# Weight products of a two-layer diffusion trunk as single matmuls on plain float32 operands, in place of three passes over split operands

## The chip, the core and the metric

The kernel runs on one core of one Trainium2 chip. The metric is the device time of one execution in microseconds (us), the median of several runs. Its engines are TensorE (PE in the profile, its weight loads PEld), VectorE (DVE), ScalarE (ACT), GpSimd (POOL) and SyncE (SP), which issues nearly all DMAs.

## The reference

Two layers are applied to 1152 tokens (128 context tokens and 1024 latent grid tokens, nine tiles of 128) of width 1024. Each layer is:

```
m = silu(c) @ w_ada + b_ada                  -> sh1, sc1, g1, sh2, sc2, g2
z = (x * (1 + sc1) + sh1) @ w_in             (1024 -> 2336: HGRN, MLA and GQA parts)
mixed = [HGRN2 scan | MLA attention | GQA attention]
x = layernorm(ALPHA * x + g1 * (mixed @ w_out))
gate, up = (x * (1 + sc2) + sh2) @ w_ffn_in  (1024 -> 2 x 2816)
x = layernorm(ALPHA * x + g2 * ((silu(gate) * up) @ w_ffn_out))
```

Context tokens attend to themselves alone; latent tokens attend to 128 cached tokens and to all latent tokens. All inputs, outputs and weights are float32.

## The kernel before

A layer goes through four stages, in code `phase_b` to `phase_e`.

- In-projection and HGRN (`phase_b`). Activations lie transposed in `HT`, three tiles of 8 feature blocks x 384 tokens. The part `hq` is made in feature layout: 6 accumulations of 8 products with 384 moving columns. Seven further chunks of 256 columns and one of 288 are made token tile by token tile (`token_chunk`): 9 accumulations of 8 products each. The HGRN scan over nine blocks (`hgrn`) runs among them; each block has eight levels, each of which goes through VectorE, ScalarE, GpSimd, TensorE and VectorE again (lines 628 to 657), and these levels' matmuls (line 652) as well as those of lines 676, 679 and 686 are on plain float32 tiles already.
- Attention (`phase_c`): 24 + 24 groups of two query tiles; scores (line 799), softmax, turned probabilities (line 820), products with the values (line 869). Small weight products of MLA stand among them.
- Output projection (`phase_d`): two halves x nine token tiles x 8 products with 512 moving columns, the first norm, and `make_hT`, which turns and modulates the activations for the next stage.
- Feed-forward (`phase_e`): 22 blocks of 128 hidden features. `inp` makes gate and up: 2 x 3 accumulations of 8 products with 384 moving columns per block. `outp` adds the down projection of a pair of blocks: 18 accumulations with 512 moving columns.

The adaLN products (`ada`, a generator) are called between these pieces with `fill`: the parts 2 to 5 of the first layer in the first `phase_b` (64 products with 512 moving columns), all six of the second layer in the first `phase_e` (96 products). The parts 0 and 1 of the first layer come at the start (`ada0`, 32 products).

Precision is kept by splitting. `wsplit` (line 121) loads a weight tile into one of two `raw` buffers, ScalarE rounds it to float32r (line 103), and VectorE or GpSimd subtracts to get the rest (line 104); activations are split in the same way where they are made. `mm3` (line 106) issues three matmuls for each product:

```
nc.tensor.matmul(out, ah, bh, start=i == 0, stop=False)
nc.tensor.matmul(out, ah, bl, start=False, stop=False)
nc.tensor.matmul(out, al, bh, start=False, stop=i == n - 1)
```

For the adaLN products two matmuls do, since the four stationary columns hold both halves of the two condition vectors (line 184); a small matmul with `fold` adds them up (lines 193 and 201). Line 193 is called for two parts x two halves x two layers, eight times; its operands are plain float32, with 4 partitions, 2 stationary and 512 moving columns.

The order of the instructions on each engine comes from a scheduler that works by a simulated timeline of the program as it stands, so that a change of any instruction can move others. A matmul on PE waits in that order, and what is behind it waits with it.

Of the kernel before, what the change touches and what calls it, by code (L numbers as in the profile page):

```python
# [34 lines left out]
# per phase the eighths of a turned tile (mod 4) whose scaling and rounding VectorE does, and whose rest Pool does  # L35
HT_MODES = {"start": ((1, 3), (1,), (1, 3)), "D": ((1, 3), (1,), (1, 3)), "E": ((1, 3), (1,), (1, 3))}
# [17 lines left out]
class Build:  # L54
# [43 lines left out]
    def split(self, hi, lo, src, eng=None, vec=False):  # L98
        """hi = src rounded to float32r, lo = the exact rest."""
# [30 lines left out]
    def setup(self):  # L130
        nc, A = self.nc, self.A
        self.open("dram", space=DRAM)
        for p in ("const", "raw", "wsp", "M", "tmp", "small"):
            self.open(p)
# [5 lines left out]
        self.fold = self.t(c, [4, 2], tag="fold")  # L140
# [3 lines left out]
        cs = self.t(c, [P, 8, 2], tag="cs")  # L144
        nc.scalar.activation(cs, cT, AF.Silu)
        self.cs = self.t(c, [P, 160], F32R, tag="csr")
        nc.vector.memset(self.cs.bitcast(F32), 0.0)
        v = self.cs[:, :32].rearrange("p (k c) -> p k c", c=4)
        self.split(v[:, :, 0:2], v[:, :, 2:4], cs)
# [3 lines left out]
    def floors(self):  # L153
        """the second layer's lower bounds of the gates, and one minus them."""
# [19 lines left out]
    def ada(self, l, part):  # L174
        """part: 0 sh1, 1 sc1, 2 g1, 3 sh2, 4 sc2, 5 g2. A generator of eight pieces of work."""
        nc, A = self.nc, self.A
        for h in range(2):
            acc = self.ps("D")
            c0 = part * D + h * 512
            for k in range(0, 8, 2):  # L180
                hi, lo = self.wsplit(A["w_ada"][l, k * P:(k + 2) * P, c0:c0 + 512].rearrange("(a p) c -> p a c", p=P), [2, 512])
# [5 lines left out]
            m = self.tmp()  # L187
            nc.vector.tensor_copy(m[0:4, :], acc[0:4, :])
            if part in (2, 5):
                r = self.tmp()  # L190
                nc.sync.dma_start(r[0:2, :], A["b_ada"][l:l + 1, c0:c0 + 512].broadcast_to([2, 512]))
                o = self.ps("D")
                nc.tensor.matmul(o[0:2, :], self.fold, m[0:4, :], start=True, stop=True)
                nc.vector.tensor_tensor(r[0:2, :], r[0:2, :], o[0:2, :], op=ALU.add)
                nc.sync.dma_start(self.gd[l][part // 3][:, h * 512:(h + 1) * 512], r[0:2, :])
                continue
            bias = self.t("small", [P, 4], tag="bada", bufs=2)
            nc.sync.dma_start(bias, A["b_adaT"][l, :, part * 8 + 4 * h:part * 8 + 4 * h + 4])
            o = self.ps("D")
            for j in range(4):  # L200
                nc.tensor.matmul(o[:, 2 * j:2 * j + 2], m[0:4, j * P:(j + 1) * P], self.fold, start=True, stop=True)
# [6 lines left out]
    def ada0(self):  # L208
        """the first layer's sh1 and sc1."""
# [4 lines left out]
        def finish(part, h, m):  # L214
            o = self.ps("D")
            for j in range(4):
                nc.tensor.matmul(o[:, 2 * j:2 * j + 2], m[0:4, j * P:(j + 1) * P], self.fold, start=True, stop=True)
# [6 lines left out]
        for part in range(2):  # L224
            for h in range(2):
                acc = self.ps("D")
                c0 = part * D + h * 512
                for k in range(0, 8, 2):
                    w = self.t("st", [P, 2, 512], tag="w", bufs=16)
                    nc.sync.dma_start(w, A["w_ada"][0, k * P:(k + 2) * P, c0:c0 + 512].rearrange("(a p) c -> p a c", p=P))  # L230
                    hi, lo = (self.t("st", [P, 2, 512], F32R, tag=g, bufs=2) for g in "hl")
                    self.split(hi, lo, w)
                    for a in range(2):
                        for x in (hi, lo):
                            nc.tensor.matmul(acc, self.cs[:, 4 * (k + a):4 * (k + a) + P], x[:, a],
                                             start=k + a == 0 and x is hi, stop=k + a == 7 and x is lo)
                    if k == 0 and todo:
                        finish(*todo)
                if part == 0 and h == 0:
                    nc.sync.dma_start(self.ident, A["ident"])  # L240
                    nc.sync.dma_start(self.still, A["still"])
                    nc.sync.dma_start(self.fold, A["fold"])
                    nc.sync.dma_start(bias, A["b_adaT"][0, :, 0:16])
                m = self.tmp()
                nc.vector.tensor_copy(m[0:4, :], acc[0:4, :])
# [8 lines left out]
    def coefs(self, l, which, ln):  # L254
        """(scale, shift) [P, 8, 2] of the modulation; with ln = (layer, norm) that norm's gain and bias are in them."""
# [12 lines left out]
    def make_hT(self, coefs, ci, xt, dst, phase):  # L268
# [3 lines left out]
        vec, hi, pool = HT_MODES[phase]  # L272
        for k in range(8):
# [3 lines left out]
            tm = self.tmp("tu"[k % 2])  # L277
            segs = [(0, P, 0), (P, 384, 1)] if ci == 0 else [(0, 384, 1)]
            for a, b, v in segs:
                if k % 4 in vec:  # L280
                    nc.vector.tensor_scalar(tm[:, a:b], ps[:, a:b], sc[:, k, v:v + 1], sh[:, k, v:v + 1],
                                            op0=ALU.mult, op1=ALU.add)
                else:
                    nc.scalar.activation(tm[:, a:b], ps[:, a:b], AF.Identity, scale=sc[:, k, v:v + 1], bias=sh[:, k, v:v + 1])
# [3 lines left out]
    def hts(self, t, k, a):  # L288
        return self.HT[t // 3][:, k, a, (t % 3) * P:(t % 3 + 1) * P]

# [1 line left out]
    def stats(self, u):  # L292
        """one over the deviation, and the mean, of the rows."""
# [10 lines left out]
    def norm(self, u):  # L304
        """layer norm without gain and bias, in place."""
# [6 lines left out]
    def ln_rows(self, ln):  # L312
        """gain and bias rows of a norm on all partitions [P, 2, D]."""
# [4 lines left out]
    def gate_rows(self, l, gi, dst):  # L318
        """dst [P, 2, D]: the gate rows of both vectors on all partitions."""
# [1122 lines left out]
```

## Time and profile before

| | |
|---|---|
| median of 3 runs | 4151.19 us (4141.76 to 4161.65) |
| profiled execution, first to last instruction | 4234.5 us |
| PE busy | 3772.9 us (89%) |
| DVE, ACT, POOL busy | 53%, 37%, 31% |
| HBM read and written | 231.05 MB, 38.87 MB (64 GB/s over the span) |

The profiled execution has no other time of its own than its span; it is 83 us over the median of the runs. Of the first layer, the in-projection and HGRN lie at about 60 to 460 us of the span, the attention at 460 to 1170, the output projection at 1170 to 1290, the feed-forward at 1290 to 2180; the second layer follows at about 2180, 2570, 3260 and 3400.

In the profile's rows for PE a matmul's duration is from its start to the modelled end of its pipeline, so that the durations of successive matmuls overlap. How long one holds the engine is the distance between two successive starts. A granted clock (PEclk) of 1.00 is 2.4 GHz and 0.50 is 1.2 GHz; a stretch with a value between has had both.

### The profile page before, as it was taken

The page shows a single profiled execution, that of the slowest core. Times are in us where ns is not written, and L with a number is a line of the kernel's source. Part 1 is how long each engine was busy: PE and PEld are TensorE (multiplying, and loading weights), DVE is VectorE, ACT ScalarE, POOL GpSimd, SP SyncE. Part 2 cuts the span into 40 slices and gives each one's busy share as a digit, 9 for nine tenths or more (in the row PEclk, how much of TensorE's full clock was granted, in tenths as well). Part 3 has the DMA queues.
Part 4 walks back from the last instruction along what each step waited for, and adds up shares of the span by engine and source line. Part 5 has one row for each costly group of instructions (what it writes and reads, how often), then busy time and mean ns, then how long its engine had stood idle before and what let it go on. Part 6 is the DMA issues. An engine that isn't in the chain of part 4 may idle for free. (4 is left out here: it accounts for less than half of the span.)

```text
span 4234.5 us, 58490 instructions
## 1 busy us (share of the span) xinstructions
PE 3772.9 (89%) x21820; PEld 3429.4 (81%) x21820; DVE 2251.7 (53%) x4256; ACT 1587.9 (37%) x3576; POOL 1330.6 (31%) x1558
## 2 busy tenths in 40 slices
PE   8999867777799999999999987777777999999997
PEld 7987756677679899999989877666766799999996
DVE  5688355555566434443366883654544743333336
ACT  5543455555433122122144335655553421111111
POOL 1277552232126000000432876513222650000043
PEclk9988988988899999999999988888888999999999
DMA  6322533211224222222331114221112221111121
GB/s 213 111 74 63 142 43 41 25 15 14 42 69 137 73 75 80 65 75 72 104 123 57 52 45 106 48 37 21 14 20 59 74 93 50 40 45 45 40 90 70
DMA packets 235207, 282.13 MB, mean 67 GB/s; under 512 B 98057, under 2 KB 163721, under 8 KB 234538
## 3 DMA queue, kind: packets, MB, share of 16 engines
q1 hardware_dynamic: 234922, 278.38, 24.9%
q8 instruction: 172, 2.82, 0.3%
q14 instruction: 113, 0.93, 0.1%
HBM read 231.05 MB, written 38.87 MB: 64 GB/s over the span
## 5 line engine op out<-in xcount | busy, mean ns | idle before, releaser
L111 PE MATMUL b<-h,w 128*128 128x384 f32 x1848 | 623.5, 337 | 5.2 <-DVE h L104 5.2
L112 PE MATMUL b<-h,w 128*128 128x384 f32 x1848 | 623.2, 337 | 2.1 <-DVE w L104 2.1
L110 PE MATMUL b<-h,w 128*128 128x384 f32 x1848 | 624.1, 338 | 0.4 <-ACT w L103 0.4
L104 DVE TENSOR_TENSOR w<-raw,w 128x1024 fp32r<-128x1024 f32 (+2 forms) x268 | 342.1, 1285 | 397.6 <-ACT w L103 337.6
L103 ACT CAST w<-raw 128x1024 fp32r<-128x1024 f32 (+2 forms) x272 | 281.4, 1039 | 675.7 <-PE b L111 236.2
L1258 POOL TENSOR_TENSOR acc<-acc,lg 128x512 f32<-128x512 f32 x36 | 50.8, 1428 | 1283.7 <-DVE acc L1244 1278.9
L111 PEld LDWEIGHTS b<-h,w 128*128 128x128 f32 x1848 | 348.5, 189 | 11.5 <-DVE h L104 6.4
L110 PEld LDWEIGHTS b<-h,w 128*128 128x128 f32 x1848 | 348.3, 189 | 9.9 <-issue 2.6
L112 PEld LDWEIGHTS b<-h,w 128*128 128x128 f32 x1848 | 348.5, 189 | 6.0 <-DVE w L104 2.4
L820 PE MATMUL c<-ident,p 128*128 128x128 f32 x1728 | 308.2, 302 | 35.6 <-ACT px L824 16.2
L104 DVE TENSOR_TENSOR pt<-c,pt 128x512 fp32r<-128x512 f32 (+2 forms) x404 | 240.4, 603 | 155.4 <-ACT pt L103 150.8
L110 PE MATMUL a<-w,h 128*128 128x256 f32 (+1 forms) x960 | 285.2, 297 | 2.9 <-ACT st L406 1.1
L103 ACT CAST pt<-c 128x512 fp32r<-128x512 f32 (+2 forms) x404 | 206.8, 526 | 211.3 <-PE c L820 180.2
L820 PEld LDWEIGHTS c<-ident,p 128*128 128x128 f32 x1728 | 231.5, 156 | 63.3 <-ACT px L824 19.8
L111 PE MATMUL a<-w,h 128*128 128x256 f32 (+1 forms) x960 | 282.6, 294 | 0.0
L112 PE MATMUL a<-w,h 128*128 128x256 f32 (+1 forms) x960 | 281.9, 294 | 0.0
L771 POOL TENSOR_TENSOR m<-u 64x256 f32<-64x256 f32 (+1 forms) x120 | 80.3, 669 | 621.0 <-DMA u<-u 555.1
L869 PE MATMUL d<-pt,V 128*128 128x256 f32 x864 | 202.0, 342 | 72.1 <-POOL pt L826 44.3
L800 DVE TENSOR_REDUCE m<-b 128x1 f32<-128x384 f32 x356 | 195.0, 553 | 117.2 <-PE b L799 114.9
L869 PE MATMUL d<-pt,v 128*128 128x256 f32 x864 | 188.7, 330 | 62.5 <-DVE u L873 21.6
L805 ACT ACTIVATE p<-b,nm 128x384 f32<-128x384 f32 x356 | 205.2, 585 | 98.5 <-DVE nm L803 77.5
L869 PEld LDWEIGHTS d<-pt,V 128*128 128x128 f32 x864 | 147.2, 221 | 87.1 <-POOL pt L826 49.9
(395 smaller groups left out, 9451.7 us busy)
## 6 DMA issues: line engine op xcount, KB each, us to landing
raw<-in_w_ffn_in_dram SPq DMA_DIRECT2D x88, 512.0 KB, 3.5
raw<-in_w_ada_dram SPq DMA_DIRECT2D x80, 512.0 KB, 3.8
raw<-in_w_ffn_out_dram SPq DMA_DIRECT2D x44, 512.0 KB, 4.7
raw<-in_w_in_a_dram SPq DMA_DIRECT2D x32, 512.0 KB, 3.9
rb<-rind SPq DMA_DIRECT2D x96, 128.0 KB, 5.1
xs<-acc SPq DMA_DIRECT2D x36, 256.0 KB, 4.1
u<-xs SPq DMA_DIRECT2D x36, 256.0 KB, 3.1
w<-in_w_ada_dram SPq DMA_DIRECT2D x16, 512.0 KB, 6.7
```

Of the source, the lines that this page charges most:

```text
L103: self.nc.scalar.copy(hi, src)
L104: (eng or self.nc.vector).tensor_tensor(lo, src, hi.bitcast(F32), op=ALU.subtract)
L110: self.nc.tensor.matmul(out, ah, bh, start=i == 0, stop=False)
L111: self.nc.tensor.matmul(out, ah, bl, start=False, stop=False)
L112: self.nc.tensor.matmul(out, al, bh, start=False, stop=i == n - 1)
L771: nc.gpsimd.tensor_tensor(self.mx(hd // 2)[r:r + 64, cols], On[r:r + 64], sw[r:r + 64], op=ALU.add)
L800: nc.vector.reduce_max(mx[:, c:c + 1], ps, axis=AX.X)
L805: nc.scalar.activation(pt[:, c * 384:(c + 1) * 384], tiles[c], AF.Exp, bias=nm, accum_out=sm[:, i, c:c + 1])
L820: nc.tensor.transpose(pt[:, (2 * a + i) * P:(2 * a + i + 1) * P], g["p"][i][:, kt * P:(kt + 1) * P], self.ident)
L869: nc.tensor.matmul(po[:, :256], g["v"](kt), w[:, i, a * 256:(a + 1) * 256], start=kt == 0 and i == 0, stop=kt == 8 and i == 1)
L1258: nc.gpsimd.tensor_tensor(acc[t][:, hs], acc[t][:, hs], g[:, min(t, 1)], op=ALU.mult)
```

## The change

Weights, transposed activations and the adaLN condition are kept as plain float32 tiles and go into one matmul per product (`mm` in place of `mm3`). `wsplit` becomes `wload`, a load straight into a ring of ten tiles; the `raw` buffers are gone. `make_hT` writes its result into `HT` in one step per segment, on VectorE for odd and ScalarE for even feature blocks. `phase_d` uses the attention's outputs as they lie. `ada` uses two stationary columns and needs no `fold`. The HGRN scan, the scores and the products with the values are as before, with their own splits.

```diff
-    def mm3(self, out, terms):
+    def mm(self, out, terms):
         n = len(terms)
-        for i, (ah, al, bh, bl) in enumerate(terms):
-            self.nc.tensor.matmul(out, ah, bh, start=i == 0, stop=False)
-            self.nc.tensor.matmul(out, ah, bl, start=False, stop=False)
-            self.nc.tensor.matmul(out, al, bh, start=False, stop=i == n - 1)
+        for i, (a, b) in enumerate(terms):
+            self.nc.tensor.matmul(out, a, b, start=i == 0, stop=i == n - 1)
...
-    def wsplit(self, src, shape, eng=None):
-        raw = self.t("raw", [P] + shape, F32, tag="raw", bufs=2)
-        self.nc.sync.dma_start(raw, src)
-        hi = self.t("wsp", [P] + shape, F32R, tag="w", bufs=8)
-        lo = self.t("wsp", [P] + shape, F32R, tag="w", bufs=8)
-        self.split(hi, lo, raw, eng)
-        return hi, lo
+    def wload(self, src, shape):
+        w = self.t("wsp", [P] + shape, F32, tag="w", bufs=10)
+        self.nc.sync.dma_start(w, src)
+        return w
...
     def ada(self, l, part):
...
-                    for w in (hi, lo):
-                        nc.tensor.matmul(acc, self.cs[:, 4 * (k + a):4 * (k + a) + P], w[:, a],
-                                         start=k + a == 0 and w is hi, stop=k + a == 7 and w is lo)
+                    nc.tensor.matmul(acc[0:2, :], self.cs[:, k + a, :], w[:, a], start=k + a == 0, stop=k + a == 7)
...
     def make_hT(self, coefs, ci, xt, dst):
...
-            tm = self.tmp("tu"[k % 2])
...
-                if k % 4 in vec:
-                    nc.vector.tensor_scalar(tm[:, a:b], ps[:, a:b], sc[:, k, v:v + 1], sh[:, k, v:v + 1],
+                if k % 2:
+                    nc.vector.tensor_scalar(dst[:, k, a:b], ps[:, a:b], sc[:, k, v:v + 1], sh[:, k, v:v + 1],
                                             op0=ALU.mult, op1=ALU.add)
...
-            self.split(dst[:, k, 0, :], dst[:, k, 1, :], tm[:, :384], eng=nc.gpsimd if k % 4 in pool and ci < 2 else nc.vector,
-                       vec=k % 4 in hi)
...
-                m = self.t("r2", [P, 8, 2, P], F32R, tag="mxs", bufs=2)
+                m = self.t("r2", [P, 2, P], tag="mxs", bufs=2)
...
-                self.split(m[:, 2:6, 0], m[:, 2:6, 1], ka[:, :, sl])
-                self.split(m[:, 6:8, 0], m[:, 6:8, 1], kb[:, :, sl], eng=nc.gpsimd)
+                nc.scalar.copy(m, ps[:, :256].rearrange("p (j s) -> p j s", j=2))
...
-                hi, lo = self.wsplit(A["w_ffn_in"][l, f, which], [8, P])
+                w = self.wload(A["w_ffn_in"][l, f, which], [8, P])
...
-                    self.mm3(ps[:, :384], [(hi[:, k], lo[:, k], self.HT[ci][:, k, 0, :], self.HT[ci][:, k, 1, :]) for k in range(8)])
+                    self.mm(ps[:, :384], [(w[:, k], self.HT[ci][:, k, :]) for k in range(8)])
...
-                        self.split(act[:, 0, sl], act[:, 1, sl], g)
+                        nc.vector.tensor_tensor(act[:, sl], gs[:, sl], ps[:, :384], op=ALU.mult)
```

TensorE's order changes in two ways. The first place is the feed-forward of the second layer, at the step from one token block to the next; `h` are the activations, `w` the weights, `b` the PSUM bank. Before:

```order
L110 MATMUL b_35501<-h_6840_31816,w_35469 128x384
L111 MATMUL b_35501<-h_6840_31816,w_35469 128x384
L112 MATMUL b_35501<-h_6840_31816,w_35470 128x384
L110 MATMUL b_35529<-h_7020_32865,w_35469 128x384
L111 MATMUL b_35529<-h_7020_32865,w_35469 128x384
L112 MATMUL b_35529<-h_7020_32865,w_35470 128x384
```

Now, where x8 is eight such rows in succession:

```order
L108 MATMUL b_26089<-h_6320_24248,w_26087 128x384 x8
L108 MATMUL b_26099<-h_6321_24249,w_26087 128x384 x8
L108 MATMUL d_26109<-h_6469_24840,w_26087 128x384 x8
L108 MATMUL b_26123<-h_6320_24248,w_26121 128x384 x8
L108 MATMUL b_26133<-h_6321_24249,w_26121 128x384 x8
```

Twenty-four rows for an accumulation have become eight; the accumulations stand in the same order.

The second place is the end of the HGRN scan of the second layer. `Q` and `X` are the operands of a level, `tx` a tile of queries and keys that is turned, `K` and `Q` of line 799 (769 now) the attention's. Before, the last level:

```order
L652 MATMUL b_23037<-Q_23034,X_23028 128x128 x2
L111 MATMUL a_24493<-w_24181,h_4084_20196 128x256
L652 MATMUL b_23041<-Q_23034,X_23028 128x128 x2
L112 MATMUL a_24493<-w_24180,h_4084_20196 128x256
L110 MATMUL a_24493<-w_24180,h_4084_20196 128x256
```

Now, from the last two levels on:

```order
L622 MATMUL b_16405<-Q_16402,X_16396 128x128 x2
L622 MATMUL b_16409<-Q_16402,X_16396 128x128 x2
L622 MATMUL b_16422<-Q_16419,X_16413 128x128 x2
L622 MATMUL b_16426<-Q_16419,X_16413 128x128 x2
L649 MATMUL c_16436<-it_16202,at_16206 128x64 x2
L646 MATMUL c_16436<-Sf_14724,m_14221 128x128
L649 MATMUL c_16436<-it_16202,at_16206 128x64 x2
L501 MATMUL c_17127<-ident_72,tx_17124 128x128
L501 MATMUL c_17137<-ident_72,tx_17133 128x128 x4
L501 MATMUL c_17171<-ident_72,tx_17167 128x128 x4
L501 MATMUL c_17205<-ident_72,tx_17201 128x128 x4
L769 MATMUL b_17745<-K_4363_17099,Q_17098 128x384
```

Before, in-projection products are left when the scan ends; now they have been moved in among the scan's levels. In the whole order, 240 products stand between the first and the last level of the first layer before and 320 now; in the second layer 247 and 339. The adaLN products between them are 16 before (32 matmuls) and 27 now.

## Rows read from the trace of the kernel before

**Rows 1.** The page: busy time, and the chain that ended last.

```profile
PE 3772.9 (89%) x21820; PEld 3429.4 (81%) x21820; DVE 2251.7 (53%) x4256; ACT 1587.9 (37%) x3576; POOL 1330.6 (31%) x1558
PE 21%; DVE 2%; DMA 2%; POOL 0%; ACT 0%; issue 0%; SPq 0%; POOLq 0%; DVEq 0%; ACTq 0%
```

**Rows 2.** Windows: stretch, length, busy time (instructions) by engine, granted clock, DMA share, GB/s.

```profile
0.00:106.00 106.00, 93.61 (x565) 82.77 (x566) 60.74 (x89) 57.02 (x93) 15.60 (x14) 0.97 0.63 213
212.00:318.00 106.00, 103.38 (x690) 90.26 (x690) 90.57 (x205) 42.56 (x87) 79.00 (x100) 0.87 0.25 74
318.00:424.00 106.00, 95.61 (x594) 81.76 (x593) 92.66 (x209) 42.23 (x85) 81.48 (x108) 0.82 0.21 64
1060.00:1166.00 106.00, 74.63 (x410) 68.73 (x411) 53.55 (x123) 48.38 (x132) 21.10 (x26) 0.81 0.28 46
1166.00:1272.00 106.00, 104.57 (x470) 82.48 (x468) 65.34 (x115) 37.90 (x74) 27.20 (x36) 0.98 0.20 65
1272.00:1378.00 106.00, 101.00 (x556) 95.45 (x556) 69.68 (x77) 40.60 (x58) 67.97 (x46) 0.98 0.44 139
2332.00:2438.00 106.00, 99.11 (x737) 88.10 (x737) 94.70 (x221) 41.05 (x93) 87.69 (x117) 0.94 0.16 51
2438.00:2544.00 106.00, 95.57 (x636) 84.61 (x635) 85.60 (x198) 41.00 (x88) 82.08 (x116) 0.84 0.15 47
```

**Rows 3.** Windows: 630 us of the second layer's feed-forward.

```profile
3500.00:4130.00 630.00, 630.00 (x3369) 596.22 (x3368) 221.04 (x300) 101.44 (x155) 50.59 (x36) 1.00 0.16 51
```

**Rows 4.** Groups of that stretch: engine, operation, tiles, shapes, count, busy us, mean ns.

```profile
L110 PE MATMUL b<-h,w 128*128 128x384 f32 x627 | 210.8, 336 | 0.0
L110 PE MATMUL d<-h,w 128*128 128x384 f32 x208 | 69.9, 336 | 0.0
L110 PE MATMUL a<-w,m 128*128 128x512 f32 x144 | 56.1, 389 | 0.0
L110 PE MATMUL c<-w,m 128*128 128x512 f32 x144 | 56.1, 389 | 0.0
```

**Rows 5.** Timeline of PE, split matmuls: start us, duration us, operation, tiles, shapes.

```profile
74.42 0.28 PE L110 MATMUL a<-w,h 128*128 128x256 f32 x1
...
76.29 0.28 PE L111 MATMUL a<-w,h 128*128 128x256 f32 x1
...
3544.81 0.39 PE L110 MATMUL a<-w,m 128*128 128x512 f32 x1
...
3549.80 0.39 PE L111 MATMUL c<-w,m 128*128 128x512 f32 x1
...
3599.94 0.34 PE L110 MATMUL d<-h,w 128*128 128x384 f32 x1
...
3609.30 0.34 PE L110 MATMUL b<-h,w 128*128 128x384 f32 x1
```

**Rows 6.** Timeline of PE: eight adaLN matmuls in succession.

```profile
76.52 2.01 PE L184 MATMUL d<-w,csr 128*128 128x512 f32 x8
```

**Rows 7.** Line 193 (durations ns min/median/max), and one call of it in the timeline.

```profile
L193 PEld LDWEIGHTS d<-t,fold x16: 75/76/78, 104.3 to 2072.2; 4*2 4x2 f32 x16
L193 PE MATMUL d<-t,fold x16: 585/586/587, 104.3 to 2072.6; 4*2 4x512 f32 x16
2072.22 1.01 PE L193 MATMUL d<-t,fold 4*2 4x512 f32 x2
```

**Rows 8.** Line 686, two blocks of it in the timeline, and windows over these.

```profile
L686 PE MATMUL c<-it,m x144: 270/275/580, 197.6 to 2521.0; 128*128 128x128 f32 x144
211.25 1.05 PE L686 MATMUL c<-it,m 128*128 128x128 f32 x8
331.23 2.07 PE L686 MATMUL c<-it,m 128*128 128x128 f32 x8
331.20:333.30 2.10, 2.10 (x10) 1.85 (x9) 2.10 (x5) 0.73 (x2) 2.02 (x4) 0.50 0.00 0
```

**Rows 9.** The costliest group of the splits on VectorE.

```profile
L104 DVE TENSOR_TENSOR w<-raw,w 128x1024 fp32r<-128x1024 f32 (+2 forms) x268 | 342.1, 1285 | 397.6 <-ACT w L103 337.6
```

More of the change, by code (lines that the diff above doesn't have):

```diff
@@ L132, in setup @@
         self.open("dram", space=DRAM)
-        for p in ("const", "raw", "wsp", "M", "tmp", "small"):
+        for p in ("const", "wsp", "M", "tmp", "small"):
             self.open(p)
@@ L139, in setup @@
         self.still = self.t(c, [P, 1], tag="still")
-        self.fold = self.t(c, [4, 2], tag="fold")
+        self.two = self.ident[0:2, 0:2]
         self.adac = [self.t(c, [P, 4, 8, 2], tag=f"adac{l}") for l in range(L)]
@@ L143, in setup @@
         nc.sync.dma_start(cT, A["cT"])
[L144 to L149, printed above, removed]
+        self.cs = self.t(c, [P, 8, 2], tag="cs")
+        nc.scalar.activation(self.cs, cT, AF.Silu)
         self.xs = self.t("dram", [NT, P, D], tag="xs")
@@ L200, in ada @@
             for j in range(4):
-                nc.tensor.matmul(o[:, 2 * j:2 * j + 2], m[0:4, j * P:(j + 1) * P], self.fold, start=True, stop=True)
+                nc.tensor.matmul(o[:, 2 * j:2 * j + 2], m[0:2, j * P:(j + 1) * P], self.two, start=True, stop=True)
             dst = self.adac[l][:, {0: 0, 1: 1, 3: 2, 4: 3}[part], 4 * h:4 * h + 4]
@@ L216, in finish @@
             for j in range(4):
-                nc.tensor.matmul(o[:, 2 * j:2 * j + 2], m[0:4, j * P:(j + 1) * P], self.fold, start=True, stop=True)
+                nc.tensor.matmul(o[:, 2 * j:2 * j + 2], m[0:2, j * P:(j + 1) * P], self.two, start=True, stop=True)
             dst = self.adac[0][:, part, 4 * h:4 * h + 4]
@@ L230, in ada0 @@
                     nc.sync.dma_start(w, A["w_ada"][0, k * P:(k + 2) * P, c0:c0 + 512].rearrange("(a p) c -> p a c", p=P))
-                    hi, lo = (self.t("st", [P, 2, 512], F32R, tag=g, bufs=2) for g in "hl")
-                    self.split(hi, lo, w)
                     for a in range(2):
-                        for x in (hi, lo):
-                            nc.tensor.matmul(acc, self.cs[:, 4 * (k + a):4 * (k + a) + P], x[:, a],
-                                             start=k + a == 0 and x is hi, stop=k + a == 7 and x is lo)
+                        nc.tensor.matmul(acc[0:2, :], self.cs[:, k + a, :], w[:, a], start=k + a == 0, stop=k + a == 7)
                     if k == 0 and todo:
@@ L266, in coefs, with make_hT @@
         return o[:, 0], o[:, 1]
[L268 removed]
+    def make_hT(self, coefs, ci, xt, dst):
         nc = self.nc
         sc, sh = coefs
[L272 removed]
         for k in range(8):
@@ L356, in token_chunk @@
                 ps = self.ps("A")
-                terms = [(self.hts(t, k, 0), self.hts(t, k, 1), hi[:, k - k0, :], lo[:, k - k0, :])
-                         for k0, k1, hi, lo in ws for k in range(k0, k1)]
-                self.mm3(ps[:, :n], terms)
+                self.mm(ps[:, :n], [(self.hts(t, k), w[:, k - k0, :]) for k0, k1, w in ws for k in range(k0, k1)])
                 evac(t, ps)
@@ L455, in phase_b @@
                 ps = self.ps("A")
-                terms = [(hi[:, k - k0, j * P:(j + 1) * P], lo[:, k - k0, j * P:(j + 1) * P],
-                          self.HT[ci][:, k, 0, :], self.HT[ci][:, k, 1, :])
-                         for k0, k1, hi, lo in ws for k in range(k0, k1)]
-                self.mm3(ps[:, :384], terms)
+                self.mm(ps[:, :384], [(w[:, k - k0, j * P:(j + 1) * P], self.HT[ci][:, k, :]) for k0, k1, w in ws for k in range(k0, k1)])
                 sg = stage()
@@ L915, in mla_turn @@
         nc, A, z = self.nc, self.A, self.z
[L916 to L917 removed]
+        mqT = self.t("mA", [P, 2, TOK], tag="mqT")
+        cT = self.t("mA", [P, 10, P], tag="ckvT")
         kE = self.t("mA", [P, 2, 10, P], F32R, tag="kE0")
[L919 removed]
+        rot = self.t("wsp", [P, 1024], tag="w", bufs=10)
         nc.sync.dma_start(rot, A["rope_feat"])
[L921 to L922 removed]
+        uq = [self.wload(A["w_uq"][l, k], [768]) for k in range(2)]
+        ukv = self.wload(A["w_ukv"][l], [768])
         self.mla = mqT, cT, rot, uq, ukv, [kE]
@@ L1036, in prep_k @@
             r = slice(e * 64, e * 64 + 64)
-            w = [ukv[a][:, pr * P:(pr + 1) * P] for a in range(2)]
             kf = kE[e].rearrange("p a t s -> p a (t s)")
             ps = self.ps("S")
-            self.mm3(ps[:, :n], [(w[0], w[1], cf[:, 0, c:c + n], cf[:, 1, c:c + n])])
+            self.mm(ps[:, :n], [(ukv[:, pr * P:(pr + 1) * P], cf[:, c:c + n])])
             x = self.tmp()
@@ L1065, in prep_q @@
             sl = slice(t0 * P, t0 * P + n)
-            self.mm3(ps[:, :n], [(uq[k][0][:, hd * P:(hd + 1) * P], uq[k][1][:, hd * P:(hd + 1) * P], mqT[:, k, 0, sl], mqT[:, k, 1, sl])
-                                 for k in range(2)])
+            self.mm(ps[:, :n], [(uq[k][:, hd * P:(hd + 1) * P], mqT[:, k, sl]) for k in range(2)])
             tm = self.tmp("t")
@@ L1140, in phase_d @@
         self.open("ht")
-        self.HT = [self.t("ht", [P, 8, 2, 384], F32R, tag=f"h{i}") for i in range(2)]
+        self.HT = [self.t("ht", [P, 8, 384], tag=f"h{i}") for i in range(2)]
         self.open("r2")
@@ L1149, in phase_d @@
         for half in range(2):
-            ws = [self.wsplit(A["w_out"][l, half, kp], [2, 512]) for kp in range(4)]
+            ws = [self.wload(A["w_out"][l, half, kp], [2, 512]) for kp in range(4)]
             for t in range(NT):
                 sl = slice(t * P, (t + 1) * P)
-                m = self.t("r2", [P, 8, 2, P], F32R, tag="mxs", bufs=2)
+                m = self.t("r2", [P, 2, P], tag="mxs", bufs=2)
                 ps = self.ps("T")
@@ L1231, in outp @@
                     ps = self.ps("T")
-                    self.mm3(ps, [(a[:, sl], b[:, sl], c[:, hs], d[:, hs]) for a, b, c, d in ops])
+                    self.mm(ps, [(a[:, sl], w[:, hs]) for a, w in ops])
                     if first:
@@ L1280, in after @@
             if l < L - 1 and t in (2, 5):
-                self.make_hT(cf, t // 3, acc, self.HT[t // 3], "E")
+                self.make_hT(cf, t // 3, acc, self.HT[t // 3])
         prev = None
@@ L1302, in phase_e @@
             self.open("ht")
-            self.HT = [self.t("ht", [P, 8, 2, 384], F32R, tag=f"h{i}") for i in range(2)]
+            self.HT = [self.t("ht", [P, 8, 384], tag=f"h{i}") for i in range(2)]
         self.open("r2")
@@ L1334, in run @@
         self.open("ht")
-        self.HT = [self.t("ht", [P, 8, 2, 384], F32R, tag=f"h{i}") for i in range(2)]
+        self.HT = [self.t("ht", [P, 8, 384], tag=f"h{i}") for i in range(2)]
         self.open("ht2")
-        self.HT.append(self.t("ht2", [P, 8, 2, 384], F32R, tag="h2"))
+        self.HT.append(self.t("ht2", [P, 8, 384], tag="h2"))
         for ci in range(3):
-            self.make_hT(self.coefs(0, 0, None), ci, x, self.HT[ci], "start")
+            self.make_hT(self.coefs(0, 0, None), ci, x, self.HT[ci])
         self.close("acc")
@@ L1391, in layout @@
     o["ident"] = np.eye(P, dtype=f)
-    o["fold"] = np.array([[1, 0], [0, 1], [1, 0], [0, 1]], f)
     i, j = np.arange(P)[:, None], np.arange(P)[None, :]
```

63 lines of the change are left out of this document (25 added, 38 removed).

## The prediction

> **What bounds the kernel now.** I read the page first. PE is busy for 89% of the span and leads the chain that ended last, while VectorE has 53%; the chain is PE in nearly all of what it names [rows 1]. An average hides the stages, so the windows come next. In the feed-forward PE is busy for 630.0 of 630 us at a granted clock of 1.00, and VectorE for 221 [rows 3]: the stage is bound by TensorE alone. The output projection is nearly so, 104.6 of 106 us [rows 2]. The attention is not: 74.6 of 106, clock 0.81. In the HGRN scan PE is busy for 103.4 and 95.6 of 106, but so is VectorE for 90.6 and 92.7, GpSimd for 79.0 and 81.5, and the clock is 0.87 and 0.82; there a chain through four engines sets the pace, and PE has slack [rows 2].
>
> Busy PE is not yet PE at its peak, so I took distances between starts from the timeline [rows 5]. For the split matmuls: 512 moving columns, 3549.80 - 3544.81 over 22 steps, 0.227 us; 384 columns, 9.36 us over 54 steps, 0.1733; 256 columns, 1.87 over 16 steps, 0.117. From 384 to 512 columns it is 0.0534 us for 128, 0.417 ns a column, one column per cycle at 2.4 GHz; 13 ns are left over per matmul. These distances fill the stretch: 3 x 835 matmuls of 384 columns and 3 x 288 of 512 (the groups of lines 111 and 112 are as large as those of line 110) [rows 4] make 434 + 196 = 630 us. So time in the feed-forward is PE's count times these distances, nothing else.
>
> **What one product costs after.** Plain float32 matmuls are in the trace already. Line 193 has eight calls and 16 records: one instruction runs as two records, each with a weight load [rows 7]. With 512 columns a record takes 0.586 us against 0.389 for a split one of the same width [rows 4], and two of them take 1.01, so the second starts 0.427 us after the first, 1024 columns at 2.4 GHz. A record therefore streams the columns twice, and a product four times in all, where the split form streams them three times. Line 193 has few weights (2 columns); line 686 has full ones, 128 x 128, with 128 columns: eight records (four matmuls) take 1.05 us, less 0.27 for the last, over 7 is 0.111 us, again 2 x 128 columns (0.107) and 5 ns more [rows 8]. I take 2N/2.4 ns + 5 ns for a record, from line 686 because its weights have the shape of these. The ends are 0 (line 193) and the split form's 13 ns.
>
> A product of 512 columns goes from 0.680 to 0.863 us (+0.183), 384 from 0.520 to 0.650 (+0.130), 256 from 0.351 to 0.436 (+0.085). For 288 columns there is no row; an estimate between the neighbours is +0.097. An adaLN product is two matmuls now, (2.01 - 0.39) / 7 = 0.231 us apart [rows 6], and takes two records of 0.427 after: +0.39.
>
> **The sum, by stages.**
> Feed-forward: 2 layers x 22 x 2 x 3 x 8 = 2112 products of 384 columns, +275 us; 2 x 22 x 18 = 792 of 512, +145; 96 adaLN products in the first layer, +37. All of it is on the path: +457.
> Output projection: 2 x 144 x 0.183 = +53. Here splits go from VectorE and ScalarE, and PE idles 1.4 us in one window and 5 in the next [rows 2]; I give 8 back: +45.
> In-projection and HGRN: all its products, 1008 x 0.085 + 144 x 0.097 + 96 x 0.130 + 64 x 0.39, are +137 on PE. But the scan's slack takes some, and the order puts more into it. In the first layer 240 products and 16 adaLN ones (84 + 7 us) between its first and last level become 320 and 27 (140 + 23): +72 us inside. The slack is idle 2.6 + 10.4 us and half of the time at 1.2 GHz, (0.13 + 0.18) x 2 x 106 / 2 = 33 us, for the two windows of the scan's 280 us: about 46, if denser work keeps the clock up. That leaves +26. In the second, 247 to 339 products make 87 into 148 us; its slack is 6.9 + 10.4 idle and 23 from the clock, 40: +21. Outside the scan there are fewer products and costlier ones, so that little remains: -7 for both layers. Together +40. The ends are -30 (the scan shortens, since VectorE loses its weight splits: 240 products and 16 adaLN ones take some 15 tiles of 1285 ns [rows 9], 19 us, in the second layer about 9) and +137 (no slack at all).
> Attention: some 72 MLA products of 512 columns and smaller ones, about +14 on an engine that idles 31 us in 106; I take +5.
> Start and passages between stages: PE idles 12 us in the first 106 [rows 2], waiting in part for roundings that are gone; each `make_hT` has one step less. -15, between 0 and -30.
> The splits themselves, among them 342 us of VectorE in one group [rows 9], lie beside PE's work where PE is full, and give nothing there.
> Together 457 + 45 + 40 + 5 - 15 = +532 us. On the profiled execution's 4234.5 us that makes 4767. It was 83 us over the median of the runs, and its feed-forward is filled by matmul distances that an unprofiled run has too, so I add the microseconds rather than scale them: 4151 + 532 = 4683, rounded to 4685.
>
> The range's ends: without the 5 ns 3192 products of feed-forward and projection lose 10 ns each, -31; with the scan's stage at -30 in place of +40 and the passages at -30 that is 4683 - 31 - 70 - 15, about 4570. With 13 ns per record +51, with the in-projection all exposed +97: about 4835.
>
> A page of the Trainium skill speaks against this. "Perfetto Trace Analysis", section "Engine Utilization", lets the array's output rate halve for FP32_LOW_HIGH, and halve only. Taken for a whole product, it would make the plain form two passes against three, and the change a gain. The trace agrees with the halving for one record, 0.427 us for 512 columns, but it shows two records to a product.
>
> **Rivals.**
> 1. Two passes to a product (what that rule would give). Line 193 with its 2 weight columns and line 686 with 128 moving ones might be cases in which a product is run twice, and wide products not. Then 512 columns cost 0.427 for 0.680, 384 0.320 for 0.520, 256 0.213 for 0.351: 2112 x -0.200, 792 x -0.253, 288 x -0.253 are -695, and about 500 products outside the scan -70, since the scan stays. Some 3390 us, faster. It decides as soon as the distance per product at 384 columns is under 0.52. For it: no row has a plain product both wide and full. Against it: both shapes in the trace, which have nothing else in common, give four passes, to 5 ns. 2%.
> 2. The weights show. Two loads a product might cost the split form's 13 ns a record: +51 on feed-forward and projection, 17 ns for each of 1248 products more in the in-projection, +21; and the costlier products would then leave the scan no slack. 4740 to 4835, say 4790. For it: the split matmuls leave 13 ns at every width. Against: line 686 leaves 5. 16%.
> 3. More is given back. The scan gets shorter without weight splits on VectorE and with its clock at 1.00, and the passages lose all they can: 4570 to 4640, say 4600. For it: VectorE is busy for 81 to 89% of those windows [rows 2]. Against: GpSimd at 79 to 88 of 106 us in the same windows [rows 2], which the change leaves alone. 10%.
> 4. Plain products at 1.2 GHz throughout. Line 686 does take 2.07 us for 1.05 in a window with clock 0.50 [rows 8], but the block at 211 us takes half of that among other matmuls, and at 331 us PE had just been in a stretch with idle time, which the feed-forward doesn't have. It would add 2112 x 0.65 + 792 x 0.86, some 2050 us, in the feed-forward alone: about 6700. 1%.
> That the change doesn't do what it says is excluded for PE: the order shows one matmul to a product.
>
> **How the numbers follow.** The forecast, 4640 to 4740 us, has 58%; with rivals 2 and 3 the range 4570 to 4835 holds 84%. Rival 1 has 2% and rival 4 1%; the other 13% are terms that I have not seen, more of them above the range than below, and nearly all still slower than before. Faster by over 0.5% (under 4130; 0.5% is about what a measurement of this kernel tells from no change): 2% for rival 1 and 1% for an unknown. Within 0.5%: 1%. Slower: 96%.
>
> **What the profile after would show.** In the feed-forward: two records per product, 0.325 us apart at 384 columns and 0.43 at 512, and PE busy for all of the time. Twice 0.16 would mean rival 1; 0.333 and 0.44 rival 2. Line 172's adaLN records stand 0.427 apart. The attention keeps its length to within 15 us. From the scan's first to last level about 280 to 320 us in each layer, with a granted clock nearer to 1.00 than 0.82. VectorE's share falls from 53% to near 40%, without effect. The forecast is wrong if the two feed-forwards together lengthen by less than 400 or more than 520 us.

## The result, and the profile after

The changed kernel takes 4679.97 us (median of 3 runs, 4679.32 to 4683.90) against 4151.19: ratio 1.1276 [1.1235, 1.1317], 529 us slower. The forecast was 4685 (range 4570 to 4835). The total is right, but in part by luck: two terms of the sum were 60 us too high together, and a third 57 too low. The rest of this text is mostly about these.

The profiled execution of the changed kernel has a span of 4677.5 us. From its page, busy time and the chain that ended last, as in [rows 1]:

```profile
PE 4307.5 (92%) x17196; PEld 2760.9 (59%) x17196; DVE 1689.4 (36%) x3654; ACT 1186.9 (25%) x3015; POOL 1170.2 (25%) x1486
PE 24%; DMA 1%; DVE 1%; issue 0%; ACT 0%; POOL 0%; SPq 0%; POOLq 0%; DVEq 0%
```

VectorE falls from 53% to 36%, ScalarE from 37% to 25%, and PE, the one that counts, rises by 535 us. Against the second profile of the kernel before (first experiment; span 4149.1 us, PE busy for 3740.3) it rises by 567, and the time that PE idles falls by 39: together the 528 us by which the span grows.

Groups of the changed kernel in 540 us of the second layer's feed-forward, columns as in [rows 4]; below them the window over it (stretch, length, busy time by engine, granted clock, DMA share, GB/s), and PE's timeline in it (start, duration) with one row from the start:

```profile
L108 PE MATMUL b<-h,w 128*128 128x384 f32 x816 | 268.9, 486 | 0.0
L108 PE MATMUL c<-w,m 128*128 128x512 f32 x216 | 97.1, 592 | 0.0
L108 PE MATMUL a<-w,m 128*128 128x512 f32 x216 | 97.1, 592 | 0.0
L108 PE MATMUL d<-h,w 128*128 128x384 f32 x285 | 96.8, 486 | 0.0
```

```profile
3900.00:4440.00 540.00, 540.00 (x1533) 291.01 (x1532) 93.73 (x143) 16.20 (x33) 0.00 (x0) 1.00 0.11 34
```

```profile
129.77 1.89 PE L108 MATMUL a<-w,h 128*128 128x256 f32 x8
...
3999.64 7.90 PE L108 MATMUL b<-h,w 128*128 128x384 f32 x24
4007.38 3.17 PE L108 MATMUL a<-w,m 128*128 128x512 f32 x7
```

Over the whole kernel there are 3696 records of `b<-h,w` of this width, where lines 110, 111 and 112 had 1848 each, one of each to a product. So a product is two records. The distance between their starts is (7.90 - 0.486) / 23 = 0.322 us at 384 columns, (3.17 - 0.592) / 6 = 0.430 at 512, (1.89 - 0.379) / 7 = 0.216 at 256. These fill the stretch: 816 + 285 records at 0.3223 and 432 at 0.4295 make 540.4 of 540 us. A product of 384 columns now costs 0.645 us (0.520 before, [rows 5]), one of 512 0.859 (0.680). The four passes are there.

Where the 529 us lie is read from first and last starts of a few lines. For the changed kernel (line, count of records: duration in ns, first and last start):

```profile
L622 PE MATMUL b<-qT,X x72: 272/272/373, 203.2 to 469.1; 64*128 64x128 f32 x72
L622 PE MATMUL b<-Q,X x504: 272/272/373, 207.5 to 496.4; 64*128 64x128 f32 x168
L790 PE MATMUL c<-ident,p x864: 270/272/476, 554.1 to 1167.0; 128*128 128x128 f32 x173
L1179 ACT ACTIVATE gate<-b x66: 487/491/492, 1308.1 to 2352.7; 128x384 f32<-128x384 f32 x66
...
L622 PE MATMUL b<-qT,X x72: 272/272/373, 2573.5 to 2828.9; 64*128 64x128 f32 x72
L622 PE MATMUL b<-Q,X x504: 272/272/373, 2574.0 to 2849.8; 64*128 64x128 f32 x168
L790 PE MATMUL c<-ident,p x864: 270/272/476, 2895.7 to 3497.8; 128*128 128x128 f32 x173
L1179 ACT ACTIVATE gate<-b x55: 486/491/491, 3640.2 to 4580.0; 128x384 f32<-128x384 f32 x55
```

For the kernel before, from a second profiled execution (span 4149.1 us, the first experiment):

```profile
L652 PE MATMUL b<-qT,X x72: 272/272/580, 173.2 to 410.4; 64*128 64x128 f32 x72
L652 PE MATMUL b<-Q,X x504: 272/272/580, 174.3 to 440.8; 64*128 64x128 f32 x168
L820 PE MATMUL c<-ident,p x864: 270/272/477, 492.4 to 1125.7; 128*128 128x128 f32 x173
L1212 ACT ACTIVATE gate<-b x66: 467/490/494, 1255.1 to 2077.8; 128x384 f32<-128x384 f32 x66
...
L652 PE MATMUL b<-qT,X x72: 272/272/580, 2263.3 to 2475.8; 64*128 64x128 f32 x72
L652 PE MATMUL b<-Q,X x504: 272/272/580, 2264.4 to 2500.3; 64*128 64x128 f32 x168
L820 PE MATMUL c<-ident,p x864: 270/273/475, 2545.7 to 3167.3; 128*128 128x128 f32 x173
L1212 ACT ACTIVATE gate<-b x55: 471/490/494, 3298.4 to 4061.6; 128x384 f32<-128x384 f32 x55
```

The stages between these marks (first scan level, last level, last turned probability, first SiLU, next layer's first level), in us:

| stage | before | after | difference |
|---|---|---|---|
| start, up to the first scan level | 173.2 | 203.2 | +30.0 |
| scan, layer 1 / 2 | 267.6 / 237.0 | 293.2 / 276.3 | +25.6 / +39.3 |
| attention, 1 / 2 | 684.9 / 667.0 | 670.6 / 648.0 | -14.3 / -19.0 |
| output projection, 1 / 2 | 129.4 / 131.1 | 141.1 / 142.4 | +11.7 / +11.3 |
| feed-forward 1 and in-projection 2 | 1008.2 | 1265.4 | +257.2 |
| feed-forward 2 and end | 850.7 | 1037.3 | +186.6 |

The sum is +528.4. Feed-forward and what lies with it have 444 of it. Each kernel has one profile here, so a difference of a few us in a stage may be chance; the first experiment says how far such stages repeat.

### The profile page after: what moved, and what is told of

It is laid out like the page before. It is cut to its first block, busy times and chain, and to the rows that moved or that the text cites. A ratio compares the mean times of both kernels' runs of the same rounds, so it can differ in the third digit from the quotient of the medians.

```text
span 4677.5 us, 47944 instructions
## 1 busy us (share of the span) xinstructions
PE 4307.5 (92%) x17196; PEld 2760.9 (59%) x17196; DVE 1689.4 (36%) x3654; ACT 1186.9 (25%) x3015; POOL 1170.2 (25%) x1486
## 5 line engine op out<-in xcount | busy, mean ns | idle before, releaser
L108 PE MATMUL b<-h,w 128*128 128x384 f32 x3696 | 1222.3, 487 | 0.0
L108 PEld LDWEIGHTS b<-h,w 128*128 128x128 f32 x3696 | 697.9, 190 | 521.8 <-issue 64.7
L108 PE MATMUL a<-w,h 128*128 128x256 f32 (+1 forms) x1920 | 468.2, 391 | 3.2 <-DVE st L404 1.5
L108 PEld LDWEIGHTS a<-w,h 128*128 128x128 f32 x1920 | 352.2, 191 | 83.4 <-issue 14.7
L108 PE MATMUL c<-w,m 128*128 128x512 f32 x816 | 366.3, 593 | 0.2 <-DVE xg L1202 0.2
L108 PE MATMUL a<-w,m 128*128 128x512 f32 x768 | 344.8, 593 | 0.0
L1182 DVE TENSOR_TENSOR m<-gate,b 128x384 f32<-128x384 f32 x110 | 61.0, 554 | 732.5 <-PE b L108 732.5
L108 PEld LDWEIGHTS c<-w,m 128*128 128x128 f32 x816 | 154.3, 190 | 184.5 <-issue 170.7
L108 PEld LDWEIGHTS a<-w,m 128*128 128x128 f32 x768 | 145.3, 190 | 175.6 <-issue 165.6
L1208 DVE TENSOR_TENSOR acc<-acc,c 128x512 f32<-128x512 f32 x144 | 99.0, 688 | 258.2 <-PE c L108 258.2
```

The costliest lines, as they stand in the source:

```text
L108: self.nc.tensor.matmul(out, a, b, start=i == 0, stop=i == n - 1)
L1182: nc.vector.tensor_tensor(act[:, sl], gs[:, sl], ps[:, :384], op=ALU.mult)
L1208: nc.vector.tensor_tensor(acc[t][:, hs], acc[t][:, hs], ps, op=ALU.add)
```

## The experiments

Each run is compared with runs of the kernel before that were taken with it (median 4155.04, 4152.61 or 4144.85 us).

**Was the first profile a longer execution?** The kernel before, unchanged.

> The kernel before, unchanged, for a second profile. The first profiled execution was 4234.5 us, 83 over the median of its runs; the one of the changed kernel was 4677.5, 2 under its median. Theory: those 83 us belong to that one execution (its attention stages were 719 and 711 us from the scan's end to the last turned probabilities), so this profile's span is 4140 to 4180 and its attention some 30 to 40 us shorter per layer. Rival: profiling always costs this kernel 2%, so the span is 4210 to 4250 again, with attention stages of 710 to 720.

4153.09 against 4155.04 us, 0.9991 [0.9974, 1.0008], with a span of 4149.1. So the first profile's 83 us over the median belonged to that one execution; its attention stages lasted 719 and 711 us by the same marks, against 685 and 667 here. Adding microseconds to the median instead of scaling was right, and stages are compared with this second profile. Three of the runs below leave the attention as it was (feed-forward alone, output projection alone, four passes): theirs last 683 to 684 and 667 to 673 us. So the marks repeat within about 6 us; what made the first execution's attention longer is not known.

**One part at a time.** One source holds both forms, with a switch for each of adaLN (A), in-projection (B), MLA (C), output projection (D) and feed-forward (E); its weight ring has eight buffers, as before the change, where the changed kernel has ten. Two hunks of the diff:

```diff
+PL = dict(A=0, B=0, C=0, D=0, E=1)
...
-                    self.mm3(ps[:, :384], [(hi[:, k], lo[:, k], self.HT[ci][:, k, 0, :], self.HT[ci][:, k, 1, :]) for k in range(8)])
+                    if PL["E"]:
+                        self.mm(ps[:, :384], [(w[:, k], self.HT[ci][:, k, :]) for k in range(8)])
+                    else:
+                        self.mm3(ps[:, :384], [(hi[:, k], lo[:, k], self.HT[ci][:, k, 0, :], self.HT[ci][:, k, 1, :]) for k in range(8)])
```

Feed-forward alone (E):

> Only the feed-forward's products (gate, up, down) are plain; all else is split as before. Theory (PE's count times distance, no slack): 2112 products x 0.130 + 792 x 0.183 = +420 us by the prediction's 5 ns per record, +405 by the distances of the changed kernel's trace (0.322 us per record at 384 columns, 0.4295 at 512): 4555 to 4571. Rival, part is given back since the splits leave VectorE and ScalarE: +300 to +350.

4521.89 against 4155.04, 1.0878 [1.0856, 1.0900]: +367. By its profile the two feed-forward stages grow by 190.6 and 187.4 us, where the distances give 202.5 each (half of 2112 x 0.1246 + 792 x 0.179). The total lies between theory and rival. The mechanism holds; 7% is given back, 12 us in the first layer and 15 in the second. In the last stage PE's idle time at the start (4.1 us in 50) goes, and 4.5 us less of it are left in the last 120; the rest was not followed.

In-projection alone (B):

> Only the in-projection's products are plain. Theory, the scan has slack on PE and takes up products that stood behind it: +40 us, between -30 and +70. Rival, no slack: 1008 x 0.085 + 144 x 0.097 + 96 x 0.130 = +112.

4212.45 against 4155.04, 1.0136 [1.0113, 1.0160]: +57. The scans grow by 25 and 41 us, the attentions shrink by 26 and 9; the start is 10 longer, the stretch from the first SiLU to the second scan 18.

Output projection alone (D):

> Only the output projection's products are plain. The prediction has +45 of a sum of 53 on PE; the changed kernel's trace has its two stages longer by 12 and 8 us, +20. Theory now: +20, because before PE waited there for the mixed activations' splits. Rival: all of 53 shows.

4172.35 against 4155.04, 1.0045 [1.0030, 1.0060]: +17, where PE's added work is 52. The windows over the first layer's projection stage, in the kernel before (second profile) and in this one:

```profile
1125.70:1255.10 129.40, 124.33 (x568) 99.82 (x568) 82.68 (x141) 51.95 (x97) 35.09 (x44) 0.96 0.25 75
```

```profile
1121.60:1261.40 139.80, 139.79 (x412) 69.49 (x411) 58.87 (x101) 33.13 (x57) 17.06 (x27) 1.00 0.19 62
```

PE idles 5.1 us before, 5.0 of it until the split of the mixed activations is done, and runs at a clock of 0.96; without the splits it idles 0.0 at 1.00. These are two reserves that a busy share of 96% does not show. Of the 26 us of work added in this stage 10 show; idle time and clock (0.04 of 129 us) are worth 10 of the 15 that don't, and the rest was not followed.

MLA products alone (C):

> Only the weight products of MLA's queries, keys and values are plain. The prediction has +5 for them. Against the kernel before's second profile, the changed kernel's attention is 14 and 19 us shorter. Theory A: the plain MLA products make it so (their splits on ScalarE and VectorE were in the attention's chain): -15 to -35. Theory B: the attention is shorter because in-projection products no longer stand in its first 100 us, and MLA's own cost shows: 0 to +14.

4141.13 against 4152.61, 0.9975 [0.9954, 0.9996]: -11, between the two theories. By the profile each attention is 5 us shorter, about as far as such marks repeat; with a total whose interval just leaves out zero, MLA's splits seem to be worth a little more there than its dearer products cost.

adaLN alone (A):

> Only the adaLN products are plain (two records of 512 columns at 0.43 us where two matmuls at 0.231 were). Theory, on the path wherever PE is full: 96 in the first feed-forward x 0.396 = +38, 64 in the first in-projection of which the scan's slack hides half, +13, 32 at the start beside the weight loads, 0 to +13: +50 to +65. Rival: the sum of the parts measured so far (367 + 57 + 17 = 441) falls short of the changed kernel's +525 by 84, so if the parts add up this one and MLA's are +84 together; if they don't, +35 or less here.

4181.17 against 4152.61, 1.0071 [1.0046, 1.0096]: +29, a miss, and as the rival had it. The first layer's feed-forward has its +41.6 and the start +12, but the first scan and attention become 12 and 11 us shorter. The window over that scan:

```profile
185.50:440.80 255.30, 246.25 (x1680) 192.78 (x1679) 207.03 (x483) 93.34 (x204) 183.08 (x243) 0.98 0.22 71
```

Between its levels stand 241 in-projection and 32 adaLN products, as in the kernel before (240 and 32, window below). The adaLN products cost PE 13 us more there, and the scan is 12 shorter, at a clock of 0.98 in place of 0.87: of 21 weight tiles that VectorE subtracted in this stretch 8 are left, and 15 us of its busy time go.

**Do the weights' subtractions cost anything?** The rest is not formed, and the rounded part is used twice: as many matmuls and loads as before, one VectorE step less per weight tile. The products lack the weights' rest. The edit does two more things: a weight takes one buffer of the ring of eight where it took two, and the order of the instructions moves.

```diff
-        self.split(hi, lo, raw, eng)
-        return hi, lo
+        self.nc.scalar.copy(hi, raw)
+        return hi, hi
```

> The kernel before with its three passes, but the rests of the weights are not formed: each weight's rounded part is used in their place, so 342 us of VectorE (and some of GpSimd) go and no matmul does. Theory, splits lie beside PE's work: within 15 us of before; the feed-forwards keep 850 us to within 12. Rival, splits were on the path in part: -40 or more.

4124.16 against 4152.61, 0.9934 [0.9903, 0.9964]: -28, a miss. The windows over the first scan, in the kernel before (second profile) and in this one:

```profile
173.20:440.80 267.60, 254.52 (x1672) 219.82 (x1671) 221.77 (x500) 109.04 (x220) 189.26 (x246) 0.87 0.23 71
```

```profile
172.30:413.70 241.40, 232.66 (x1619) 200.18 (x1618) 196.56 (x476) 105.50 (x213) 177.84 (x239) 0.94 0.24 74
```

VectorE (third busy time) has 25 us less, and the scan is 26 us shorter at a higher clock. But part of this is work that moved. The in-projection's products between the levels, before and in this run (columns as in [rows 4]; two more matmuls a product):

```profile
L110 PE MATMUL a<-w,h 128*128 128x256 f32 x240 | 73.9, 308 | 1.2 <-ACT st L406 1.2
```

```profile
L110 PE MATMUL a<-w,h 128*128 128x256 f32 x222 | 66.3, 299 | 0.6 <-ACT st L405 0.6
```

Nearly 19 products, some 7 us of PE, now stand in the attention behind, which is 9 us longer. At most some 19 us of the 26 are left for the edit itself, and they need not all be the subtractions': ScalarE's wait for a weight buffer that adaLN matmuls free falls too (us in total, times, longest; before and in this run):

```profile
ACT w L103 <- PE d L184: 11.3, 9, 2.9
```

```profile
ACT w L125 <- PE d L183: 4.6, 4, 2.2
```

The two were not separated. With adaLN alone, where hardly a product moved, it comes out the same way: the splitting of weights, its buffers included, was on the first scan's path. In the second scan it is 3 us, in the feed-forwards and the in-projection between them 16 of 1859. The second projection is 13 us longer, which was not followed. Beside a PE that is full the subtractions are worth little.

**Is it the passes, or the plain type?** Split products of the feed-forward with the fourth term, rest by rest.

```diff
+            self.nc.tensor.matmul(out, al, bl, start=False, stop=False)
```

> The kernel before with a fourth split matmul per feed-forward product (rest times rest). Theory, a product costs its passes times their distance: +2112 x 0.1733 + 792 x 0.2267 = +546, about 4700; plain products make four passes in 0.645 and 0.859 us where this needs 0.693 and 0.907, so it is some 140 us over the kernel with a plain feed-forward (4522). Rival, plain products' time is not one of four passes: no relation, and a fourth pass at 384 columns could cost less than 0.17 where weights are loaded already.

4674.40 against 4152.61, 1.1248 [1.1202, 1.1293]: +522. Its timeline in the feed-forward:

```profile
4099.81 0.34 PE L109 MATMUL b<-h,w 128*128 128x384 f32 x1
4099.98 0.34 PE L110 MATMUL b<-h,w 128*128 128x384 f32 x1
4100.15 0.34 PE L111 MATMUL b<-h,w 128*128 128x384 f32 x1
4100.33 0.34 PE L112 MATMUL b<-h,w 128*128 128x384 f32 x1
4100.50 0.34 PE L109 MATMUL b<-h,w 128*128 128x384 f32 x1
```

Four passes of 0.173 us. The stages grow by 271.9 and 256.4 where passes times distance gives 273 each; the 17 us that the second lacks were not followed. Four split passes are dearer than a plain product by 152 us over the feed-forward alone, of which the distances explain 141 (0.049 us a product at either width, for 2904 products): 13 ns for each of four passes against 2 to 3 ns for each of two records.

**Do the parts add up?** Alone they make 367 + 57 + 17 - 11 + 29 = 459 of 529 (or of 525, against the 4155.04 of the first of these runs). In-projection and adaLN together (A, B), and everything but the feed-forward (A to D):

> The in-projection's and the adaLN products plain together, all else split. Alone they cost +57 and +30 us. The five parts alone add up to 460 of the changed kernel's 525; by stages 61 of what is missing lies between the start and the end of the first layer's attention (together +41 there in the changed kernel; alone the in-projection +10 and adaLN -11). Theory, the same PE slack was counted in both: each alone fits into the first scan and the time behind it, both do not. Then +130 to +150 here, with about 285 to 295 us of scan and the first three stages +35 to +45. Rival, parts add up and the rest is lost elsewhere (projection, MLA): +87.

> Everything plain but the feed-forward's products. Theory, the feed-forward shares nothing with the other stages: the changed kernel's +525 less the feed-forward's own +367 gives +158 (4312). Rival, the parts are worth their own sum: 57 + 17 - 10 + 30 = +94.

The pair takes 4264.89 against 4144.85, 1.0290 [1.0272, 1.0307]: +120, between the theories, and more than the +86 of the parts. All but the feed-forward takes 4285.57, 1.0339 [1.0325, 1.0354]: +141 against +92 for its parts, between its theories too. From the start to the first attention's end the pair is 29.6 us longer, where the parts alone gave +10 and -11. That is 30 of the 34 us by which the pair exceeds its parts; the first scan alone is +26, as in the changed kernel, where the parts gave +25 and -12. The slack that hid each part there is one slack, and it is spent once.

**A version that beats both?** MLA plain, and adaLN plain for the parts of the first layer alone that run ahead of its feed-forward:

```diff
+        pl = l == 0
...
-                hi, lo = self.wsplit(A["w_ada"][l, k * P:(k + 2) * P, c0:c0 + 512].rearrange("(a p) c -> p a c", p=P), [2, 512])
+                src = A["w_ada"][l, k * P:(k + 2) * P, c0:c0 + 512].rearrange("(a p) c -> p a c", p=P)
+                if pl:
+                    w = self.wload(src, [2, 512])
```

> A version that might beat both: split as before, but MLA's weight products plain (alone -10) and the adaLN products plain only where they stand among the first layer's in-projection (64 of 192), where VectorE and not PE sets the scan's pace: alone, with all adaLN products plain, the first scan was 12 us and the attention behind it 11 us shorter, while the first feed-forward was 42 and the start 12 longer. Expected: -10 for MLA, -15 to -23 for adaLN, together -20 to -33 (4120 to 4133). Rival, both gains are the scheduler's luck in one place: within 8 us of before.

4136.00 against 4144.85, 0.9974 [0.9958, 0.9991]. That is 9 us below the kernel before, between theory and rival, and no better than MLA alone: the first scan gives 13 us and the start takes 11.

## Why the prediction was right, and where it was not

**Four passes in two records: right.** Distances of 0.322 and 0.430 us against 0.325 and 0.43, and adaLN records (0.592 us long) as dear as any of 512 columns. Rival 1 (two passes) falls with the 0.645 us per product. Rival 2 (the weights show, 13 ns a record) falls with 2.3 ns at 384 columns (0.3223 - 768/2400) and 2.8 at 512. Rival 4 (1.2 GHz) falls with the granted clock of 1.00 in the window above.

**Feed-forward, +457: 38 too high.** By the parts' profiles it is 190.6 + 41.6 (adaLN) in the first layer and 186.6 in the second, +419, just inside the 400 to 520 set for the two. Of the 38, 15 are the rest per record (2 to 3 ns, not 5); some 27 are the give-back that ff_plain shows, for which the sum had nothing; adaLN took 5 more.

**Output projection, +45: 22 too high.** Measured +23. Eight were given back for idle time; the idle time that goes is 5 and 8 us in the two layers, and the clock that rises from 0.96 to 1.00 and from 0.95 to 0.99, some 10 us more, was left out.

**In-projection, scan, attention and start, +30: 57 too low.** This is the step that failed. The scans have 18 of the 57: +25.6 and +39.3 against +26 and +21. The first came out as said by luck, from other sizes. Its extra PE work is +64 us (99 to 163) and not +72: the text above says that 16 adaLN products (32 matmuls) stand between the levels before, but the trace has 64 matmuls of line 184 there, 32 products. For the same reason there were 21 weight tiles to subtract there (29 us) and not some 15. The slack, set at 46 us, took up some 38. The window over that scan after the change answers to the one under the subtractions:

```profile
203.20:496.40 293.20, 284.43 (x1586) 211.90 (x1587) 197.30 (x479) 93.81 (x220) 182.23 (x259) 0.99 0.24 70
```

PE has 30 us more to do by busy time and 4 less of idle, the clock rises from 0.87 to 0.99, and the weight splits that are gone had been on this stretch's path. In the second scan 6 weight tiles were subtracted, worth 3 us; PE's idle time falls from 17 to 11 us and the clock rises from 0.92 to 0.99, which takes up 22 of 61 us of work, where the sum had 40. Both became bound by PE in part; GpSimd's waits for the level matmuls in the first scan (us in total, times, longest), before (second profile) and after:

```profile
POOL X L645 <- PE b L652: 38.9, 21, 5.5
```

```profile
POOL X L615 <- PE b L622: 56.5, 19, 10.7
```

The other 39 lie outside the scans. What failed there is "Outside the scan there are fewer products and costlier ones, so that little remains: -7", with the -15 for start and passages: it put at nothing what the costlier products ahead of the scans take. There are fewer, but on the wrong side. Behind the scans in-projection products fall from 104 to 48 in the first layer and from 90 to none in the second; there the attention has slack, and it is 14 and 19 us shorter, 5 of them in each by MLA's own plain products if these count as they do alone. (The profile was to show the attention's length kept to within 15 us, and 280 to 320 us for each scan; the 19, and the second scan's 276, miss that by a little.) Ahead of the scans PE is nearly full, and few have left. In the start, by groups (line, tiles, columns, records, busy us, mean ns), before (second profile; lines 111 and 112 are as large as 110):

```profile
L110 PE MATMUL a<-w,h 128*128 128x256 f32 x232 | 64.8, 279 | 0.0
...
L184 PE MATMUL d<-w,csr 128*128 128x512 f32 x48 | 13.3, 394 | 0.0
L235 PE MATMUL c<-l,csr 128*128 128x512 f32 x24 | 12.0, 498 | 2.7 <-DVE l L104 2.7
L235 PE MATMUL c<-h,csr 128*128 128x512 f32 x24 | 11.3, 471 | 6.5 <-ACT h L103 6.5
```

and after:

```profile
L108 PE MATMUL a<-w,h 128*128 128x256 f32 x416 | 94.1, 382 | 0.0
...
L172 PE MATMUL d<-w,cs 128*2 128x512 f32 x58 | 27.3, 592 | 0.0
L217 PE MATMUL c<-w,cs 128*2 128x512 f32 x48 | 23.8, 657 | 5.2 <-DMA w<-in_w_ada_dram 5.2
L217 PE MATMUL d<-w,cs 128*2 128x512 f32 x16 | 7.0, 592 | 0.0
```

232 products of 0.351 us become 208 of 0.430, +8; 48 of 384 columns +6; adaLN goes from 112 matmuls of 0.231 (16 more of line 235 are not shown) to 122 records of 0.430, +26. That is +40, less 8 for idle time that goes (13.4 to 5.3 us of PE's): +32, measured +30. The waits for roundings did go, but 5.2 us of the 9.2 came back as a wait for the weights' DMA. Ahead of the second scan 239 products become 237: +18, and 48 of 384 columns +6; the stage's share was 257.2 - 190.6 - 41.6 = +25. So the two places ahead of the scans cost 55 us, the two behind give 33, where the sum had -17 for all of them.

**Rival 3, more given back:** its two mechanisms are real. The clock in the scan rose, the weight splits were on the first scan's path; but it put them where the products that moved in took them up again. That the splits give nothing, as the sum has it, holds beside a full PE alone. GpSimd, named against this rival as left alone, lost 160 us of busy time in all ([rows 1]), but only 7 in the first scan.

**The balance.** -38 and -22 against +57: the 3 us that remain (+532 in the sum, +529 measured) are errors that cancel, and that the total came so near is luck. What stays open is the part of the feed-forward's give-back that was not followed, how much of the first scan's gain is the subtractions' and how much the weight buffers', and the rest by which the whole exceeds its parts: 66 us, of which the pair has 34 and all but the feed-forward 49.

## What to carry to other kernels

Price a matmul form as passes times the distance between starts, and the distance from rows of the same form, even narrow ones: where the engine is full, that is within a tenth of the answer, and taking work off other engines there buys nearly nothing. Where the engine has slack, ask on which side of the latency chain the moved products stood before: taken from a stage with slack they give less than they took, and those that stay ahead of it pay nearly in full. A slack that hides each of two edits alone is one slack.

## What was not expected of the hardware

At a granted clock of 1.00 a plain matmul's record loses 2 to 3 ns over its columns and a split one 10 to 13 ([rows 5]), with weights of the same shape. In the first scan the mean granted clock is 0.87 before and 0.99 after, at nearly the same busy share of PE, 254.5 of 267.6 us and 284.4 of 293.2. And one execution of the kernel before had attention stages 78 us longer together than another, with all other stages within 5 us; the cause is open.
